# Two block sizes per step in the decay products of three recurrent heads, and reorderings in four other stages of a fused hybrid decoder layer

## The chip, the cores and the metric

The kernel runs as one program on one core of a Trainium2 chip. The metric is the device time of one execution in microseconds (us). Engines are named as the profile names them: PE is the matrix engine (TensorE), PEld its weight load, DVE the vector engine, ACT the scalar engine, POOL the GpSimd engine, SP the engine whose queue issues the DMA transfers. SBUF is the on-chip memory with 128 partitions; PSUM is the accumulator memory, eight banks of 128 x 512 f32, into which PE writes.

## The reference: what is computed

One decoder layer on x of shape 1024 x 1024 (1024 tokens, width 1024), all in f32. In the terms of the reference:

```
h = RMSNorm(x);  p = h @ W_in          # W_in: 1024 x 3584
A = dilated sliding-window attention   # 8 heads of 64, causal, table bias
R = HGRN2 recurrence                   # 4 heads of 128
x = x + RMSNorm(concat[RMSNorm(A), R] @ W_out)
x = x + RMSNorm(relu(RMSNorm(x) @ W1)^2 @ W2)    # inner width 4096
```

For each recurrent head, f_t = lb + (1 - lb) sigmoid(f_pre), k = 1 - f, and S_t = diag(f_t) S_{t-1} + k_t v_t^T, o_t = S_t^T q_t. Written without the state, token t receives from each earlier token s the product q_t . (f_{s+1} ... f_t) . k_s, channel by channel. That matrix of decayed products is what the main part of the change computes in another way. The result of the recurrence is normalised per head and multiplied by silu(gate).

## The kernel before: how it is tiled and staged

The order of all work is written out by hand. Each engine executes its own list of instructions in that order and waits at semaphores where it needs another engine. So an instruction that waits holds up everything behind it on its engine.

Products in f32 accuracy are made in three passes of a rounded format: every operand is split by `split_into` (line 81) into a high part, a copy on ACT (line 82), and a low part, a subtraction on DVE (line 83). `three_pass` (lines 86 to 88) then does high x high, low x high and high x low. Products of plain f32 operands appear in the profile as two PE records each; they are called half products here. Weights come through `w_load` and `w_split` (two raw buffers of 128 x 1024, loaded by SP).

The stages, with their time in the profiled execution:

- **Front, 0 to 56 us.** `keep_warm(n)` (line 278) issues n products of zeros, 128x256. `x_turn` (line 254) transposes a block of x on PE, ACT and DVE split it (255, 256), `x_mm` makes the first projection (value and gate of recurrent head 0) for the token groups in `groups`, into four PSUM banks `pig`. `ig_evac` (229, 230) moves a bank out: value on ACT, gate on DVE. In the trace the two take turns at a bank, each waiting for the other.
- **Recurrent heads, 56 to 325 us.** `hgrn_core(h)` computes head h. Between its parts it calls `fill(ns)`, which takes pieces of PE work from a queue of generators until their nominal cost is used up: for heads 0 to 2 the projections of the next head (`hgrn_ig`, 192 passes of 128x256, then `hgrn_qf`, 96 passes of 128x512), for head 3 an attention projection. What is left in the queue at the end of a head is issued then. The decay matrix `at` (128 x 8 x 128: eight token blocks of 128) is built by recursive halving. For each block size c in 1, 2, 4, ..., 64, `pl` is made by eight plain f32 products of 64 columns (line 392: keys x the queries in the second halves of blocks of 2c), the keys in the first halves and the queries in the second halves are multiplied by the decay over their half (396, 398), the decays are combined (402), and a predicated copy writes the 64 columns from PSUM to their places in `at` (403). Ahead of this, `pd` (377) makes the diagonal from `prod`, which the projection of f writes (367).
- **Attention, 325 to 575 us.** Steps (head, query block b): `look` makes scores and bias two steps ahead, `raise_` the exponentials one step ahead, `turn` transposes and splits, `weigh` and `finish` multiply with v. `hooks` adds work to single steps: at step 47 a transposed row block, a weight split and a bias table load. `fill` mixes in the projection of the next pair. `keys_off` (469 to 476) moves half of a pair's keys out of PSUM: one DVE multiply, two copies on ACT, two subtractions on POOL, four transfers on SP. For the second half of a pair's keys it is put off to the step with b = 7, 0 or 1 (line 875).
- **Output projection, 575 to 650 us.** A loop over eight token blocks t: `late_out`, `row_turn(t + 1)`, `residual(t - 1)`, `row_attn(t + 2)` (702, 704), `mixed_half`, `next_turn(t - 2)`, `residual_b(t - 1)`.
- **First feed-forward product, 650 to 975 us.** 1024 x 1024 x 4096 by Strassen's scheme with seven products: `mm1(q, p, ...)` (1059 to 1061) for pair q and product p, `out_p1` to `out_p7` evacuate. The operands B22, T1, T2, T4, T3 are made while pairs 0 to 4 run. `w1_sums` and `w1_split` prepare the weights of a pair, `act_plain`, `act_sums` and `act_store` form and store the activations. Buffers are handed out by small arenas (`small`, `large`), first freed, first taken.
- **Second feed-forward product, 975 to 1294 us.** 35 units of (product, pair of pairs), each of 24 passes of 128x512; `a_load(n + 3)` loads activations (1388), `prep(n + 2)` splits them. A last plain part (`fe`) adds pairs 0 and 1, and each token block is normalised, added to the residual and stored (1602 to 1622).

Of the kernel before, what the change touches and what calls it, by code (L numbers as in the profile page):

```python
# [17 lines left out]
P = 128  # L18
# [17 lines left out]
def hymba_layer(ctx, tc, x, w_in, w_out, w_ff1, w_ff2, g_pre, lb_logits, g_mix, g_post,  # L36
# [28 lines left out]
    masks = cp.tile([P, len(LEVELS), 64], U8, name="masks")  # L65
    gpre = cp.tile([P, NK], F32, name="gpre")
# [215 lines left out]
    keep_warm(3)  # L282
    for k in range(NK):
        x_turn(0, 1, k)
        keep_warm(1)
        if k == 3:
            w_split()
    w_split()
    keep_warm(2)
    for i, grp in enumerate(groups):  # L290
# [8 lines left out]
        if i == 4:  # L299
            w_split()  # L300
            ig_evac(heads[0], pms0[0], PAIRED[0])
            ig_evac(heads[0], pms0[1], PAIRED[1])
            squares(6, 2)
            rsqrt_mean(rstd0[:, 6:], ssq0[:, 6:], D, 2)
# [3 lines left out]
    V.tensor_copy(masks, mraw)  # L308
    V.tensor_tensor(out=lb, in0=lbl[:, :, 0], in1=lbl[:, :, 1], op=ALU.subtract)
# [14 lines left out]
    def hgrn_ig(h):  # L324
        hd = heads[h] = new_head(h)
        w_get(4 * h + 1)
        for t2 in range(NT // 2):
# [7 lines left out]
            ig_evac(hd, pm, (t2 * 2, t2 * 2 + 1))  # L335
# [34 lines left out]

    def hgrn_core(h, scale, after=None):
        hd = heads[h]
        inat, gate, prod, qt, kt, tot = (hd[n] for n in ("inat", "gate", "prod", "qt", "kt", "tot"))
        fill(2200 * scale)
# [8 lines left out]
        cur = tot  # L383
        fill(2300 * scale)
        for li, c in enumerate(LEVELS):
            nb = 64 // c
            qv = qt.rearrange("p (b two c) -> p b two c", two=2, c=c)
            kv = kt.rearrange("p (b two c) -> p b two c", two=2, c=c)
            av = at.rearrange("p n (b two c) -> p n b two c", two=2, c=c)
            pl = bank("s", f"pl{h}_{li}")  # L390
            for n in range(NT):
                TE.matmul(pl[:, n * 64:(n + 1) * 64], kt[:, n * P:(n + 1) * P],  # L392
                          qv[:, n * nb:(n + 1) * nb, 1, :], start=True, stop=True)
            w = T // (2 * c)
            cv = cur[:, :2 * w].rearrange("p (b two) -> p b two", two=2)
            V.tensor_tensor(out=kv[:, :, 0, :], in0=kv[:, :, 0, :],  # L396
                            in1=cv[:, :, 1:2].to_broadcast([P, w, c]), op=ALU.mult)
            V.tensor_tensor(out=qv[:, :, 1, :], in0=qv[:, :, 1, :],  # L398
                            in1=cv[:, :, 0:1].to_broadcast([P, w, c]), op=ALU.mult)
# [3 lines left out]
            V.copy_predicated(  # L403
                av[:, :, :, 1, :],
                masks[:, li].rearrange("p (b c) -> p b c", c=c).unsqueeze(1).to_broadcast([P, NT, nb, c]),
                pl.rearrange("p (n b c) -> p n b c", n=NT, c=c))
            cur = nx
            fill(2900 * scale)
# [456 lines left out]
    for s in range(n_steps):  # L865
# [9 lines left out]
        if b in (7, 0, 1):  # L875
            while put_off:
                keys_off(*put_off.pop())
# [12 lines left out]
        hooks.get(s, lambda: None)()  # L890
        fill(3400.0 - 360.0 * b if s < n_steps - 20 else 1000.0 if s < n_steps - 16 else 1300.0)
# [87 lines left out]
    def split_pair(name, src):  # L979
        hi, lo = small.get(f"{name}h", F32R), small.get(f"{name}l", F32R)  # L980
        split_into(hi, lo, src)
# [319 lines left out]
    b_split("T3", h11)  # L1301
    large.add("A")
    for q in range(2):
        out_p6(q)
# [3 lines left out]
    wide_split(2)  # L1308
    for q in range(2):
# [5 lines left out]
    w1_split(2, 2)  # L1315
    w1_load(4)
    w1_split(2, 3)
# [373 lines left out]
```

## Time and profile before

| | |
|---|---|
| median of three executions | 1299.04 us (1296.51, 1299.04, 1299.54) |
| the profiled execution | 1296.25 us, of which its span 1294.4 us |
| PE busy | 1254.5 us, 97% of the span |
| DVE busy | 857.5 us, 66% |
| ACT busy | 515.6 us, 40% |
| POOL busy | 295.5 us, 23% |
| DMA | 153.98 MB, mean 119 GB/s |

A row of the groups reads: line, engine, operation, output <- inputs, shape, number of records; then busy us and mean ns of one; then the idle time of the engine just before these instructions and who ended it. A row of the timeline reads: start in us from the beginning of the span, length in us (of the whole run of records, where it ends in x and a number), engine, line, operation, and in brackets how long the engine was idle before and who released it. In a table of windows, each engine's busy time is followed by PEclk, the share of PE's full clock that was granted.

### The profile page before, as it was taken

The numbers are of one execution on the slowest core, as the hardware profiler recorded it, in microseconds if no ns is written. First come the engines' busy times: TensorE is split into PE (matmuls) and PEld (weight loads), VectorE is DVE, ScalarE is ACT, GpSimd is POOL, SyncE is SP. The second block draws the span as 40 slices with busy tenths as digits, with TensorE's granted clock in tenths as the row PEclk, the third lists the DMA queues.
The fourth block names the chain that finished last, engine by engine and source line by source line (L and its number), as shares of the span: only waits on it lengthen the run. The fifth ranks groups of instructions, "written<-read, shape, count | busy, mean of one in ns | idle before, by whom it ended". The sixth has DMA issues, their size and how long they took to land. (4 is left out here: it accounts for less than half of the span.)

```text
span 1294.4 us, 17367 instructions
## 1 busy us (share of the span) xinstructions
PE 1254.5 (97%) x6666; PEld 1071.5 (83%) x6666; DVE 857.5 (66%) x1395; ACT 515.6 (40%) x904; POOL 295.5 (23%) x308
## 2 busy tenths in 40 slices
PE   8999999999999999899999899999999999999997
PEld 8898989988888887787877788888878888888885
DVE  5565656575665656667758566666675777688956
ACT  6612121222555555574655322222234633344412
POOL 0000000011112123134350387575541000000012
PEclk9999999999999999999999999999999999999998
DMA  5201111132223223326242345453478454434423
GB/s 204 66 17 51 33 44 38 29 86 66 82 66 82 66 82 80 127 70 221 97 148 90 138 171 179 147 179 127 142 260 333 163 195 130 156 105 131 156 75 126
DMA packets 58577, 153.98 MB, mean 119 GB/s; under 512 B 4992, under 2 KB 12928, under 8 KB 58240
## 3 DMA queue, kind: packets, MB, share of 16 engines
q1 hardware_dynamic: 58496, 152.89, 35.6%
q8 instruction: 52, 0.85, 0.3%
q14 instruction: 29, 0.24, 0.1%
HBM read 106.73 MB, written 39.85 MB: 113 GB/s over the span
## 5 line engine op out<-in xcount | busy, mean ns | idle before, releaser
L87 PE MATMUL f<-bl,ah 128*128 128x512 f32 x392 | 152.6, 389 | 0.5 <-DVE bl L83 0.5
L86 PE MATMUL f<-bh,ah 128*128 128x512 f32 x392 | 152.6, 389 | 0.0
L88 PE MATMUL f<-bh,al 128*128 128x512 f32 x392 | 152.5, 389 | 0.0
L83 DVE TENSOR_TENSOR al<-ar,ah 128x1024 fp32r<-128x1024 f32 x49 | 60.7, 1239 | 50.2 <-ACT ah L82 21.6
L87 PEld LDWEIGHTS f<-bl,ah 128*128 128x128 f32 x392 | 73.6, 188 | 16.1 <-DVE bl L83 0.8
L86 PEld LDWEIGHTS f<-bh,ah 128*128 128x128 f32 x392 | 73.6, 188 | 15.6 <-ACT acc L1471 0.4
L88 PEld LDWEIGHTS f<-bh,al 128*128 128x128 f32 x392 | 73.6, 188 | 15.1
L82 ACT ACTIVATE ah<-ar 128x1024 fp32r<-128x1024 f32 x49 | 52.3, 1067 | 53.6 <-DMA ar<-actd 28.2
L1607 POOL TENSOR_SCALAR fp<-fss 128x1 f32<-128x1 f32 x8 | 3.5, 432 | 268.3 <-ACT fd L1604 268.3
L576 DVE CUSTOM_DVE_ANT_0 p<-ps,bt 128x512 f32<-128x512 f32 (+2 forms) x84 | 44.3, 552 | 24.1 <-PE ps L574 23.9
L603 ACT ACTIVATE pth<-pt 128x512 fp32r<-128x512 f32 (+2 forms) x96 | 43.2, 486 | 41.1 <-PE pt L600 39.4
L604 DVE TENSOR_TENSOR ptl<-pt,pth 128x512 fp32r<-128x512 f32 (+2 forms) x96 | 50.2, 551 | 13.1 <-ACT pth L603 13.1
L392 PEld LDWEIGHTS pl<-qt,kt 128*128 128x128 f32 x448 | 53.7, 194 | 1.5 <-PE pm_av L88 0.9
L392 PE MATMUL pl<-qt,kt 128*128 128x64 f32 x448 | 53.8, 273 | 0.5 <-DVE qt L398 0.5
L587 ACT ACTIVATE p<-p,nm 128x128 f32<-128x128 f32 (+3 forms) x64 | 49.5, 773 | 9.2 <-DVE nm L582 6.2
L229 ACT ACTIVATE inat<-pig,rstd 128x128 f32<-128x128 f32 x32 | 11.6, 367 | 97.3 <-PE pig L88 84.2
L78 POOL TENSOR_SCALAR ms<-hss 128x8 f32<-128x8 f32 x4 | 0.8, 197 | 210.0 <-DVE hss L444 210.0
L82 ACT ACTIVATE bh<-br 128x1024 fp32r<-128x1024 f32 x28 | 29.9, 1068 | 42.6 <-PE f L88 37.3
L633 POOL TENSOR_TENSOR anat<-anat,rd 128x128 f32<-128x128 f32 x32 | 14.5, 455 | 140.4 <-DVE anat L632 136.6
L600 PE MATMUL pt<-ident,p 128*128 128x128 f32 x288 | 42.9, 276 | 3.4 <-DVE ptl L604 3.4
L1127 POOL TENSOR_TENSOR e<-x,e 128x512 f32<-128x512 f32 x14 | 20.7, 1476 | 102.0 <-DVE x L1078 102.0
L396 DVE TENSOR_TENSOR kt<-kt,tot 128x512 f32<-128x512 f32 x28 | 20.2, 722 | 35.8 <-PE pl L392 35.8
(1586 smaller groups left out, 3869.1 us busy)
## 6 DMA issues: line engine op xcount, KB each, us to landing
ar<-actd SPq DMA_DIRECT2D x49, 512.0 KB, 3.7
raw<-in_w_in_dram SPq DMA_DIRECT2D x28, 512.0 KB, 3.6
w1r<-in_w_ff_dram SPq DMA_DIRECT2D x14, 1024.0 KB, 6.5
br<-in_w_ff_dram SPq DMA_DIRECT2D x14, 1024.0 KB, 6.5
actd<-e SPq DMA_DIRECT2D x17, 768.0 KB, 4.3
actd<-e SPq DMA_DIRECT2D x11, 1024.0 KB, 4.1
xr<-in_x_dram SPq DMA_DIRECT2D x8, 512.0 KB, 8.7
raw<-in_w_out_dram SPq DMA_DIRECT2D x8, 512.0 KB, 3.7
```

The costliest lines, as they stand in the source:

```text
L82: S.activation(hi, src, AF.Copy)
L83: eng.tensor_tensor(out=lo, in0=src, in1=f32(hi), op=ALU.subtract)
L86: TE.matmul(dst, lhs[0], rhs[0], start=start, stop=False)
L87: TE.matmul(dst, lhs[0], rhs[1], start=False, stop=False)
L88: TE.matmul(dst, lhs[1], rhs[0], start=False, stop=stop)
L392: TE.matmul(pl[:, n * 64:(n + 1) * 64], kt[:, n * P:(n + 1) * P], qv[:, n * nb:(n + 1) * nb, 1, :], start=True, stop=True)
L576: V.tensor_tensor_reduce(out=pe[:, k0:k0 + n], in0=pS[:, :n], in1=bts[hd][:, o:o + n], scale=1.0, scalar=-3.0e38, op0=ALU.add, op1=ALU.max ...
L587: S.activation(pe[:, :nk], pe[:, :nk], AF.Exp, bias=nm[:, b:b + 1], accum_out=dn[:, b:b + 1])
L600: TE.transpose(pt[:, j * P:(j + 1) * P], pe[:, jj * P:(jj + 1) * P], ident)
L603: S.activation(hi, src, AF.Copy)
L604: V.tensor_tensor(out=lo, in0=src, in1=f32(hi), op=ALU.subtract)
L1127: eng[0].tensor_tensor(out=e1[:, 3], in0=a21, in1=e1[:, 2], op=ALU.add)
```

## The change

Nine edits. The parts that carry the work, first the recurrent heads 0 to 2 (head 3 keeps the old loop, with the first two `fill` calls changed as for the others):

```
+    def quarter_sets(hd, h, step, tots):
+        c = 4 ** step
+        nb = 32 // c
+        qt = hd["qt"]
+        cv = tots.rearrange("p (n b f) -> p n b f", n=NT, f=4)
+        sets = []
+        for hf in range(2):
+            q = qt[:, hf * 512:hf * 512 + 512]
+            z = slab("T", f"qs{h}_{step}{hf}", F32, (P, 4, 192))
+            n4 = slice(hf * 4, hf * 4 + 4)
+            S.activation(z[:, :, :64].rearrange("p n (g c) -> p n g c", c=c),
+                         q.rearrange("p (n g two c) -> p n g two c", n=4, two=2, c=c)[:, :, :, 1], AF.Copy)
+            z2 = z[:, :, 64:128].rearrange("p n (b two c) -> p n b two c", two=2, c=c)
+            q4 = q.rearrange("p (n b f c) -> p n b f c", n=4, f=4, c=c)
+            S.activation(z2[:, :, :, 0], q4[:, :, :, 2], AF.Copy)
+            V.tensor_tensor(out=z2[:, :, :, 1], in0=q4[:, :, :, 3],
+                            in1=cv[:, n4, :, 2:3].to_broadcast([P, 4, nb, c]), op=ALU.mult)
+            V.tensor_tensor(out=z[:, :, 128:].rearrange("p n (b w) -> p n b w", b=nb),
+                            in0=z[:, :, 64:128].rearrange("p n (b w) -> p n b w", b=nb),
+                            in1=cv[:, n4, :, 1:2].to_broadcast([P, 4, nb, 2 * c]), op=ALU.mult)
+            sets.append(z)
+        return sets, cv
     def hgrn_core(h, scale, after=None):
...
-        fill(2200 * scale)
+        ready = quarter_sets(hd, h, 0, tot) if h < HH - 1 else None
+        fill(3300 * scale)
         pd = bank("t", f"pd{h}")
...
+        if h < HH - 1:
+            fill(1200 * scale)
+            totals = slab("P", f"tot{h}")
+            for step in range(3):
+                c = 4 ** step
+                nb = 32 // c
+                sets, cv = ready
+                banks4 = []
+                for u in range(4):
+                    pl = bank("st"[u // 2], f"pl{h}_{step}{u}").rearrange("p (n q) -> p n q", n=2)
+                    for n in range(2 * u, 2 * u + 2):
+                        TE.matmul(pl[:, n % 2, :192], kt[:, n * P:(n + 1) * P], sets[u // 2][:, n % 4],
+                                  start=True, stop=True)
+                    banks4.append(pl)
+                w = T // (4 * c)
+                at_ = (0, 768, 960)[step]
+                tots = totals[:, at_:at_ + 3 * w].rearrange("p (i w) -> p i w", i=3)
+                u23, u123, nx = (tots[:, i] for i in range(3))
+                cw = cv.rearrange("p n b f -> p (n b) f")
+                q4 = qt.rearrange("p (m f c) -> p m f c", f=4, c=c)
+                k4 = kt.rearrange("p (m f c) -> p m f c", f=4, c=c)
+
+                def spread(ap, k=c):
+                    return ap.unsqueeze(2).to_broadcast([P, w, k])
+                V.tensor_tensor(out=q4[:, :, 1], in0=q4[:, :, 1], in1=spread(cw[:, :, 0]), op=ALU.mult)
+                for hf in range(2):
+                    n4 = slice(hf * 4, hf * 4 + 4)
+                    V.tensor_tensor(out=qt[:, hf * 512:hf * 512 + 512].rearrange("p (n b f c) -> p n b (f c)", n=4, f=4, c=c)
+                                    [:, :, :, 2 * c:],
+                                    in0=sets[hf][:, :, 128:].rearrange("p n (b w) -> p n b w", b=nb),
+                                    in1=cv[:, n4, :, 0:1].to_broadcast([P, 4, nb, 2 * c]), op=ALU.mult)
+                V.tensor_tensor(out=u23, in0=cw[:, :, 2], in1=cw[:, :, 3], op=ALU.mult)
+                V.tensor_tensor(out=u123, in0=cw[:, :, 1], in1=u23, op=ALU.mult)
+                V.tensor_tensor(out=nx, in0=cw[:, :, 0], in1=u123, op=ALU.mult)
+                if step < 2:
+                    ready = quarter_sets(hd, h, step + 1, nx)
+                V.tensor_tensor(out=k4[:, :, 2], in0=k4[:, :, 2], in1=spread(cw[:, :, 3]), op=ALU.mult)
+                V.tensor_tensor(out=k4[:, :, 1], in0=k4[:, :, 1], in1=spread(u23), op=ALU.mult)
+                V.tensor_tensor(out=k4[:, :, 0], in0=k4[:, :, 0], in1=spread(u123), op=ALU.mult)
+                for u, pl in enumerate(banks4):
+                    for part_, mask, c2 in ((0, masks[:, 2 * step], c), (2, masks[:, 2 * step + 1], 2 * c),
+                                            (1, near[:, step], 2 * c)):
+                        av = at[:, 2 * u:2 * u + 2].rearrange("p n (b two c) -> p n b two c", two=2, c=c2)
+                        V.copy_predicated(
+                            av[:, :, :, 1, :],
+                            mask.rearrange("p (b c) -> p b c", c=c2).unsqueeze(1).to_broadcast([P, 2, 64 // c2, c2]),
+                            pl[:, :, part_ * 64:part_ * 64 + 64].rearrange("p n (b c) -> p n b c", c=c2))
+                cur = nx
+                fill((7000, 7000, 7000)[step] * scale)
+            pl = bank("s", f"pl{h}_6")
             for n in range(NT):
-                TE.matmul(pl[:, n * 64:(n + 1) * 64], kt[:, n * P:(n + 1) * P],
-                          qv[:, n * nb:(n + 1) * nb, 1, :], start=True, stop=True)
-            w = T // (2 * c)
-            cv = cur[:, :2 * w].rearrange("p (b two) -> p b two", two=2)
-            V.tensor_tensor(out=kv[:, :, 0, :], in0=kv[:, :, 0, :],
-                            in1=cv[:, :, 1:2].to_broadcast([P, w, c]), op=ALU.mult)
-            V.tensor_tensor(out=qv[:, :, 1, :], in0=qv[:, :, 1, :],
-                            in1=cv[:, :, 0:1].to_broadcast([P, w, c]), op=ALU.mult)
-            nx = slab("P", f"tot{h}_{w}") if w > 64 else \
-                tp.tile([P, w], F32, tag=f"tot{w}", name=f"tot{h}_{w}", bufs=1)
-            V.tensor_tensor(out=nx[:, :w], in0=cv[:, :, 0], in1=cv[:, :, 1], op=ALU.mult)
-            V.copy_predicated(
-                av[:, :, :, 1, :],
-                masks[:, li].rearrange("p (b c) -> p b c", c=c).unsqueeze(1).to_broadcast([P, NT, nb, c]),
-                pl.rearrange("p (n b c) -> p n b c", n=NT, c=c))
+                TE.matmul(pl[:64, n * 64:(n + 1) * 64], kt[:, n * P:n * P + 64], qt[:, n * P + 64:(n + 1) * P],
+                          start=True, stop=True)
+            S.activation(at[:64, :, 64:], pl[:64].rearrange("p (n c) -> p n c", n=NT), AF.Copy)
+            kv, qv = (x.rearrange("p (n two c) -> p n two c", two=2, c=64) for x in (kt, qt))
+            cv = cur.rearrange("p (n two) -> p n two", two=2)
+            V.tensor_tensor(out=qv[:, :, 1], in0=qv[:, :, 1], in1=cv[:, :, 0:1].to_broadcast([P, NT, 64]), op=ALU.mult)
+            V.tensor_tensor(out=kv[:, :, 0], in0=kv[:, :, 0], in1=cv[:, :, 1:2].to_broadcast([P, NT, 64]), op=ALU.mult)
+            nx = tp.tile([P, NT], F32, tag="tot8", name=f"tot{h}_8", bufs=1)
+            V.tensor_tensor(out=nx, in0=cv[:, :, 0], in1=cv[:, :, 1], op=ALU.mult)
             cur = nx
-            fill(2900 * scale)
+            fill(3400 * scale)
```

So a step treats the block sizes c and 2c together (c = 1, 4, 16): eight products of 192 columns take the place of sixteen of 64, and twelve predicated copies of 128 columns, from four banks, the place of two of 512. Size 64 stays by itself: keys of 64 tokens, an unconditional copy on ACT. The new mask `near` is made by three small DVE operations in front. Between the steps `fill` is called with 7000 where it was called twice with 2900.

The other edits, in the order of the stages: the front; `hgrn_ig`, where the gate too is now moved out on ACT; the attention step, where put-off keys go behind `weigh`, `finish` and the hooks; the output projection; the first feed-forward product, pairs 0 to 2; the last pair's store, two units later; and the last token block, where the gain is applied to both halves after the second.

```
-    keep_warm(3)
+    keep_warm(9)
     for k in range(NK):
         x_turn(0, 1, k)
-        keep_warm(1)
-        if k == 3:
+        if k in (3, 4):
             w_split()
-    w_split()
-    keep_warm(2)
+    keep_warm(5)
...
         if i == 4:
+            ig_evac(heads[0], pms0[0], PAIRED[0])
             w_split()
-            ig_evac(heads[0], pms0[0], PAIRED[0])
...
...
-            ig_evac(hd, pm, (t2 * 2, t2 * 2 + 1))
+            for u, t in enumerate((t2 * 2, t2 * 2 + 1)):
+                S.activation(hd["inat"][:, t], pm[:, u, 0], AF.Copy, scale=rstd0[:, t:t + 1])
+                S.activation(hd["gate"][:, t], pm[:, u, 1], AF.Copy, scale=rstd0[:, t:t + 1])
...
         turn(hd, b, exped.pop(s))
-        if b in (7, 0, 1):
-            while put_off:
-                keys_off(*put_off.pop())
...
         hooks.get(s, lambda: None)()
+        if b in (7, 0, 1):
+            while put_off:
+                keys_off(*put_off.pop())
...
+        if NE <= t + 2 < NT:
+            row_attn(t + 2)
         if t > 0:
             residual(t - 1)
-        if NE <= t + 2 < NT:
-            row_attn(t + 2)
...
-    b_split("T3", h11)
+    b_open("T3")
+    for c in range(2):
+        split_into(bops["T3"][2 * c], bops["T3"][2 * c + 1], h11[:, 2 * c:2 * c + 2])
+        out_p6(c)
     large.add("A")
-    for q in range(2):
-        out_p6(q)
...
     wide_split(2)
+    wd = large.get("wd2", F32R)
+    split_into(wd[:, 0:2], wd[:, 2:4], w1raw[2][:, 2:4])
+    ops1[2]["D"] = wd
+    ops1[2][7], ops1[2][4] = halves_of((wd[:, 0:2], wd[:, 2:4]))
+    drop(w1raw.pop(2))
+    w1_load(4)
+    w1_split(2, 3)
     for q in range(2):
         out_p3(q)
     for q in range(2):
         mm1(q, 7, "b", False)
         w1_drop(q, "D")
         out_p7(q)
-    w1_split(2, 2)
-    w1_load(4)
-    w1_split(2, 3)
...
         if n == 0:
             act_sums(NPAIR - 1)
+        if n == 2:
             act_store(NPAIR - 1)
...
-            if last:
-                V.tensor_tensor(out=c, in0=c, in1=gend[:, j], op=ALU.mult)
+            if last and j:
+                for i, e in enumerate(pieces):
+                    V.tensor_tensor(out=e, in0=e, in1=gend[:, i], op=ALU.mult)
```

The zero products in front are 14 where they were 13: nine ahead of the first transposes and five behind the last, none between. The second weight split is issued after the fifth transposed block, not after the eighth.

More of the change, by code (lines that the diff above doesn't have):

```diff
@@ L65, in hymba_layer @@
     masks = cp.tile([P, len(LEVELS), 64], U8, name="masks")
+    near = cp.tile([P, 3, 64], U8, name="near")
     gpre = cp.tile([P, NK], F32, name="gpre")
@@ L308, in hymba_layer @@
     V.tensor_copy(masks, mraw)
+    first = col("lowhalf", 3)
+    V.tensor_reduce(first, mraw[:, 0:6].rearrange("p (s two) j -> p s two j", two=2)[:, :, 0], axis=AX.X, op=ALU.max)
+    V.tensor_scalar(first, first, -1.0, 1.0, op0=ALU.mult, op1=ALU.add)
+    V.tensor_tensor(out=near, in0=mraw[:, 0:6].rearrange("p (s two) j -> p s two j", two=2)[:, :, 1],
+                    in1=first.unsqueeze(2).to_broadcast([P, 3, 64]), op=ALU.mult)
     V.tensor_tensor(out=lb, in0=lbl[:, :, 0], in1=lbl[:, :, 1], op=ALU.subtract)
@@ L977, in flat, with split_pair @@
         return ap.rearrange("p a c -> p (a c)")
-    def split_pair(name, src):
+    def split_pair(name, src, eng=V):
         hi, lo = small.get(f"{name}h", F32R), small.get(f"{name}l", F32R)
-        split_into(hi, lo, src)
+        split_into(hi, lo, src, eng)
         return hi, lo
```

35 lines of the change are left out of this document (27 added, 8 removed).

## The prediction

> **What bounds the kernel now.** The busy times first: PE is busy for 97% of the span, DVE for 66%, so time goes where PE gets less to do, or where one of its few waits goes.
>
> ```profile
> PE 1254.5 (97%) x6666; PEld 1071.5 (83%) x6666; DVE 857.5 (66%) x1395; ACT 515.6 (40%) x904; POOL 295.5 (23%) x308
> ```
>
> Then the groups by form and the timeline, for what a half product costs. The step from one record to the next counts, not the length of one:
>
> ```profile
> L392 PE MATMUL pl<-qt,kt 128*128 128x64 f32 x448 | 53.8, 273 | 0.5 <-DVE qt L398 0.5
> ...
> 10.46 1.46 PE L278 MATMUL pig<-warm 128*128 128x256 f32 x6
> ...
> 72.48 1.90 PE L392 MATMUL pl<-qt,kt 128*128 128x64 f32 x16
> ```
>
> Six half products of 256 columns: (1.46 - 0.38)/5 = 0.216 us each. Sixteen of 64 columns: (1.90 - 0.27)/15 = 0.109, no cheaper than the 128-column and 1-column ones (pd x8 in 0.95). So up to 128 columns something other than the columns sets the pace.
>
> Then PE's timeline, for its waits at the places that the change touches:
>
> ```profile
> 13.29 0.38 PE L87 MATMUL pig<-wig0l,hTh 128*128 128x256 f32 x1 [0.87 <-DVE wig0l L83]
> ...
> 202.92 1.05 PE L377 MATMUL pd<-ones,prod 128*128 128x1 f32 x8 [1.02 <-DVE prod L367]
> ...
> 601.09 0.63 PE L718 MATMUL pmt<-ident,row 128*128 128x128 f32 x4 [1.49 <-DVE row L702]
> ...
> 711.52 0.47 PE L1059 MATMUL f10b<-T30h,wd0h 128*128 128x512 f32 x1 [1.37 <-DVE x L1097]
> ...
> 726.51 0.47 PE L1059 MATMUL f12d<-T40h,wd2h 128*128 128x512 f32 x1 [3.84 <-DVE x L1094]
> ```
>
> Windows, for the granted clock. Twice a wait is followed by 3.41 us at half rate, a loss of 1.7 us of PE work each:
>
> ```profile
> 137.50:140.91 3.41, 3.41 (x18) 3.41 (x18) 0.79 (x1) 0.00 (x0) 0.00 (x0) 0.50 0.54 154
> 728.01:731.42 3.41, 3.41 (x10) 2.63 (x9) 0.28 (x1) 0.00 (x0) 0.00 (x0) 0.50 0.19 68
> ```
>
> Last the timelines of DVE and ACT: the predicated copy takes 1.32 us for blocks of 1 and 2 and 0.70 to 0.74 from 4 on, one loaded operand arrives late, and at the end a multiply by the gain stands ahead of the last sum.
>
> ```profile
> 76.23 1.32 DVE L403 COPY_PREDICATED at<-masks,pl 128x512 f32<-128x512 uint8 x1
> 85.87 0.70 DVE L403 COPY_PREDICATED at<-masks,pl 128x512 f32<-128x512 uint8 x1
> ...
> 1286.05 0.68 DVE L1613 TENSOR_TENSOR acc<-acc,gend 128x512 f32<-128x512 f32 x1
> 1286.65 0.68 DVE L1602 TENSOR_TENSOR acc<-fe,acc 128x512 f32<-128x512 f32 x1
> ...
> 993.69 1.06 ACT L82 ACTIVATE ah<-ar 128x1024 fp32r<-128x1024 f32 x1 [7.63 <-DMA ar<-actd]
> ```
>
> **The change part by part.** The sum is made against the profiled execution, 1296.25 us (span 1294.4 and 1.85 around it). It is the fastest of those shown, 2.8 below the median.
>
> *Front.* x lands at once (transposes at 5.31), so nine zero products now delay it. Cold ones step 0.43 per half; before the clock opened at 7.8 some 13 of the 18 halves fit, the other 5 take 1.1: transposes from 9.1. ACT then does four copies (0.33 apart), split, copy, split: second high part ready at 12.95. DVE's low part (1.22, behind one 0.35) ends at 14.4, where PE waited until 13.29. PE works without a break from there, so +1.2. Had the clock opened 1.3 later, both versions would start about together; 2.1 earlier, the new one 1.3 later; if the pause behind the new transposes halves the clock once more, +1.7 on top. Ends: -0.3 and +2.9. [...]
>
> *Bank first, then split* (at 42 us): PE waited 0.48 for the bank; now the low weight part, behind two ACT and two DVE moves, is ready at 42.9, so -0.1. The three mask operations (about 0.7, by the 0.16 to 0.42 of rows with 8 to 256 elements) lie in 1.46 us in which DVE waits for ACT; without that cover they would cost 0.7.
>
> *Recurrent heads 0 to 2, PE.* Per head before: 7 x 16 halves x 0.111 = 12.4 us. After: 3 x 16 halves of 192 columns. Nothing shows 192; the ends are the 128- and 256-column rows, 0.112 and 0.216, and on the line between them, 0.164, gives 7.9. Size 64: 16 halves with half the weight columns, between 0.9 and 1.8, taken at 1.3. Saved: 12.4 - 9.2 = 3.2, three heads **-9.7** (ends -0.6 and -18).
>
> *Their waits.* pd waits 0.95 at 134 and 1.02 at 203 for prod, which ends about 4 us after the last f product; the fill ahead grows by 9 passes of 0.12, so both go: -2.0. With the first goes the half clock at 137.5: -1.7.
>
> *DVE in a step.* Per two sizes before: 4 multiplies of 0.69, two copies, decays: about 5.5. After, by 0.15 + 1.05 ns per element: queries 3 x 0.42, decays up to 3 x 0.42, the next sets 2 x (0.29 + 0.42), keys 3 x 0.42, and twelve copies of 128, at blocks of 1 and 2 0.44 each (a quarter of 1.17, plus 0.15), with waits among them 5.4 in all, later 4. The queries and sets lie beside the products; keys and copies come behind them, 6.5 us against 7.5 of fill. But the four banks are wanted again one by one. Counting DVE from the last f product (fr 0.2, prod 3.3, sets 6.0, w split 7.7, at 9.0, queries, decays and sets 12.7, keys 13.8) the banks are free at 15.1, 16.5, 17.9, 19.3, and PE wants them at 17.0, 17.6, 18.3, 18.9: 0.5 us of wait in head 0. In heads 1 and 2 eight gate multiplies (2.16) stand ahead of f, DVE is 1.1 late and PE waits 1.5. So **+3.5**; ends 0 and +30, by the copy's price (rival 2). The later steps have 2 us to spare. The 24 gate moves from DVE to ACT (0.37 each) lie beside 5.8 us of PE per bank. The next weights' split at the f projection, 2.4 us of DVE, now precedes the state updates (2.6); `po` comes 5.0 us after f starts, and the first state is ready at 5.2, hidden by `po`'s first half products; a further delay would be paid in full.
>
> *Keys.* One DVE multiply (0.67), two ACT copies (1.28), two POOL subtractions (2.63) and four SP transfers move behind `finish` (0.41 DVE, 0.40 POOL) for pairs 1 and 2: 0.4 later, with over 3 us until the scores read them: 0. At step 47 they also pass a transposed block (ACT 0.60, DVE 0.69), a weight split (1.06, 1.40), its SP load and the bias table's. PE's 1.03 wait at 517.8 goes, but ACT's copies now wait for DVE until 518, exponentials and pt copies come 1.4 later, and PE waits about as long for a bank at 520.5. The last transfer goes out at 522 and takes 2.5, read at 526.9. Taken 0, ends -2.5 and +1.5.
>
> *row_attn* (0.61 + 0.35) passes four residual operations (2.86): the 1.49 wait goes. Those, their POOL sums and the x2 store come 0.9 later, and with them L795 (until 604.6), which the transposes read that PE then reaches at 602.8 instead of 604.31. Taken 0, ends -1.5 and +0.5.
>
> *First feed-forward.* out_p6(0) passes T31's split (1.22 DVE): PE starts at 710.35, not 711.52; T31 is ready at 711.4, wanted 1.4 later. The wd2 split (ACT 1.05, DVE 1.22) and wf (0.6, 0.69) pass out_p3, ACT's squares and out_p7: ready at 717.5 where f12d wanted them at 722.3. What ends that wait next is out_p5, behind DVE's out_p7: 721.9, PE there at 721.1. So 726.5 becomes 722.0: **-4.5**, and the half clock at 728 goes: -1.7. Covered: w1_load(4) goes out at 717, not 711 (6.5 to land, read after 738); squares and stores of pairs 0 and 1 are 1.8 later, wanted for a buffer at 728. Ends -6.5 and -1.
>
> *Store.* Two stores (0.37 each on SP, which waited for POOL until 984.8) now follow the loads of units 4 and 5; PE's wait at 997 goes: -0.7. Buffers come free two units later, with no reader before unit 7. Ends -0.8 and +0.5.
>
> *Tail.* L1602 starts 0.60 earlier; both gain multiplies lie beside ACT and POOL (2.2 us): -0.6.
>
> Sum: 1.2 - 0.1 - 9.7 - 3.7 + 3.5 - 6.2 - 0.7 - 0.6 = -16.3, so 1296.25 - 16.3 = **1280.0 us**.
>
> **The rivals.** (1) Half products paced by columns alone: 0.216/256 is 0.84 ns per column, so 64 would step at 0.054 and two sizes at 32 x 0.054 = 1.7 against 2.6; -9.7 would become +8: 1297.7, no change. The 0.109 row speaks against it: 3 in 100. [...]
> (2) Slower: the price of a small predicated copy is per instruction. At the full 1.32 and 0.72, step 0 holds DVE 16 us, and the waits reach some 12 + 5 us per head: 1280 - 3.5 + 50 = 1326. It decides at 20 us of waits, about 1.0 us for each copy of blocks 1 and 2. Against it: multiplies of 512, 256 and 128 take 0.68, 0.42, 0.29. With smaller mishaps of the kind, 10 in 100.
> (3) 192 columns step like 256 (0.216): +9 -> 1289: 10 in 100.
> (4) The feed-forward wait moves to out_p5 and the stores and the clock still halves: 1285: 15 in 100.
> (5) Waits at the four banks vanish and size 64 is at its low end: 1275: 10 in 100. My forecast: 52.
>
> **How the numbers follow.** The forecast reaches from 1276 to 1285. With (3), (4) and (5), 1271 to 1292 holds 8 in 10 and more; rivals 1 and 2 are outside. Under 0.3% (3.9 us) cannot be told from no change. Faster 0.86, same 0.04, slower 0.10.
>
> **What would show it.** Sixteen records of 192 columns in about 2.6 us; 48 in all three steps of a head. No wait of pd; none over 1.6 at the third and fourth bank of the second step. f12d without a wait over 1. No half clock near 137 and 728. Predicated copies of 128 columns over 0.8 us would make this wrong, as would records of 192 columns over 0.2.

## The result, and the profile after

The median went from 1298.38 to 1288.72 us, a ratio of 0.9929 (95% interval 0.9917 to 0.9942): 9.7 us faster. That is inside the range of 1271 to 1292, but outside the 1276 to 1285 of the forecast itself, and little more than half of the 19 us between 1299.04 and the forecast of 1280.0. The profiled executions, 1296.25 and 1289.73 us, lie 6.5 apart: the first is faster than each of the four before, the second the slowest of the four after. The places below are taken from these two.

The first line of busy times of the kernel after:

```profile
PE 1247.8 (97%) x6524; PEld 1061.3 (82%) x6524; DVE 885.1 (69%) x1524; ACT 533.3 (41%) x967; POOL 297.8 (23%) x308
```

PE has 6.7 us less to do (1254.5 before), DVE 27.6 more. The span became 6.5 shorter, so the waits and half-rate stretches that the change was to take away were replaced by others. The timeline of PE after, first the new products, then the waits at the places of the change:

```profile
72.13 2.77 PE L425 MATMUL pl<-qs,kt 128*128 128x192 f32 x16
...
103.69 1.15 PE L465 MATMUL pl<-qt,kt 128*64 128x64 f32 x16
...
118.22 0.71 PE L533 MATMUL po<-inat,at 128*128 128x128 f32 x4 [1.13 <-DVE st L522]
...
147.38 0.92 PE L425 MATMUL pl<-qs,kt 128*128 128x192 f32 x4 [0.32 <-DVE at L457]
148.62 0.92 PE L425 MATMUL pl<-qs,kt 128*128 128x192 f32 x4 [0.31 <-DVE at L457]
149.85 0.92 PE L425 MATMUL pl<-qs,kt 128*128 128x192 f32 x4 [0.32 <-DVE at L457]
...
598.36 1.06 PE L899 MATMUL ph<-ident,esum 128*128 128x128 f32 x8 [1.92 <-DVE esum L889]
...
600.22 0.79 PE L87 MATMUL pwo<-wh,mt 128*128 128x512 f32 x1 [0.80 <-ACT mt L83]
...
715.88 0.80 PE L1155 MATMUL f12d<-T10h,ws 128*128 128x512 f32 x1 [2.55 <-DVE ws L84]
...
723.23 0.47 PE L1153 MATMUL f12d<-T40h,wd 128*128 128x512 f32 x1 [0.68 <-DVE x L1188]
```

The products of 192 columns step by (2.77 - 0.33)/15 = 0.163 us, those of 64 columns with 64 weight columns by (1.15 - 0.27)/15 = 0.059. `pd` no longer waits. But a wait of 1.13 stands ahead of `po` in heads 0 and 1, which the kernel before did not have, the 1.49 of `pmt` has become 1.92 and 0.80 at `ph` and `pwo`, and the 3.84 of `f12d` has become 2.55 and 0.68. `po` of head 0 in the kernel before:

```profile
115.76 0.60 PE L439 MATMUL po<-inat,at 128*128 128x128 f32 x4
```

Windows of the kernel after, at the place near 137 us that was at half rate before, and at the three that are at half rate now (PEclk is the number after the five engines):

```profile
137.50:140.91 3.41, 3.41 (x28) 3.41 (x27) 3.37 (x6) 1.49 (x6) 0.00 (x0) 1.00 0.57 154
517.51:524.34 6.83, 5.96 (x22) 4.87 (x21) 3.79 (x11) 2.36 (x7) 1.24 (x1) 0.50 0.82 282
599.43:606.26 6.83, 6.04 (x14) 4.73 (x15) 5.96 (x9) 2.55 (x8) 2.18 (x4) 0.50 0.08 34
715.49:718.90 3.41, 3.02 (x7) 2.44 (x8) 3.41 (x4) 0.00 (x0) 1.47 (x1) 0.50 0.00 0
```

17.1 us at half rate, where the kernel before had 10.2 and the prediction expected 3.4 to be left.

Where the 6.5 us come from, by the start of the same product in both traces (how much earlier PE gets there, place by place), and inside the heads by the steps from one PE record to the next, summed by output:

| place | predicted | traces |
|---|---|---|
| front, to the first f projection | +1.1 | -0.3 |
| heads 0 to 2: products with their bank waits (36.5 us became 30.0) | -9.7 + 3.5 = -6.2 | -6.5 |
| heads: waits of `pd`, half clock at 137 | -3.7 | -2.4 - 1.6 = -4.0 |
| heads: wait of `po` for DVE's state updates (2.3), and slower steps around it (1.5) | 0 | +3.8 |
| attention, with the keys | 0 | +0.6 |
| output projection (row_attn) | 0 | +3.2 |
| first feed-forward product | -4.5 - 1.7 = -6.2 | -1.7 |
| store | -0.7 | -1.0 |
| tail | -0.6 | -0.6 |
| sum | -16.3 | -6.5 |

### The profile page after: what moved, and what is told of

Its sections match the earlier page's. It is cut to its first block, busy times and chain, and to the rows that moved or that the text cites. A ratio compares the mean times of both kernels' runs of the same rounds, so it can differ in the third digit from the quotient of the medians.

```text
span 1287.9 us, 17288 instructions
## 1 busy us (share of the span) xinstructions
PE 1247.8 (97%) x6524; PEld 1061.3 (82%) x6524; DVE 885.1 (69%) x1524; ACT 533.3 (41%) x967; POOL 297.8 (23%) x308
## 5 line engine op out<-in xcount | busy, mean ns | idle before, releaser
L84 DVE TENSOR_TENSOR wl<-raw,wh 128x1024 fp32r<-128x1024 f32 x23 | 31.4, 1365 | 18.3 <-ACT wh L83 18.0
L694 PEld LDWEIGHTS pt<-ident,p 128*128 128x128 f32 x288 | 33.5, 141 | 9.3 <-DVE ptl L698 6.8
L711 PE MATMUL pov<-pth,v 128*128 128x256 f32 (+1 forms) x160 | 40.6, 288 | 0.0
L1574 DVE TENSOR_TENSOR acc<-f,acc 128x512 f32<-128x512 f32 x52 | 33.8, 684 | 8.3 <-PE f L89 8.3
```

The costliest lines, as they stand in the source:

```text
L84: eng.tensor_tensor(out=lo, in0=src, in1=f32(hi), op=ALU.subtract)
L694: TE.transpose(pt[:, j * P:(j + 1) * P], pe[:, jj * P:(jj + 1) * P], ident)
L711: TE.matmul(po[:, c0:256], vst, pt[j // 4][q][:, j % 4, c0:], start=j == 0 and q == 0, stop=j == nj - 1 and q == 1)
L1574: V.tensor_tensor(out=acc_at(p, i), in0=pm, in1=acc_at(p, i), op=ALU.add)
```

## The experiments

Medians of separate comparisons stand against their own runs of the kernel before, so ratios are compared: the changed kernel's is 0.9929, and 0.0010 is 1.3 us.

### The recurrent heads alone

The kernel before with this part of the change and nothing else (front, keys, output projection, feed-forward, store and tail as before).

> The kernel before with the edit of the three recurrent heads alone (the joint block sizes, the mask for them, the gate moved out on ACT, the fills); all else as before. By the places in the trace of the changed kernel, the heads became 6.6 us shorter between the first f projection (0.34 early) and the first projection of attention (6.96 early): 1298.4 - 6.6 = 1291.8. By the terms of the prediction (-9.7 - 3.7 + 3.5) it would be 1288.5. If what the heads gain were given back in the attention behind them, it would stay above 1295.

Measured: 1288.72 against 1297.49, ratio 0.9932 (0.9917 to 0.9947). In its trace the heads are 6.6 us shorter, as in the changed kernel. So by the medians the heads carry the whole gain, and the other edits together bring nothing that can be measured. By the table they sum to about zero: -0.3, -1.7, -1.0 and -0.6 against +0.6 and +3.2. The expected time was missed: the ratio is nearer to the 1288.5 by the prediction's terms than to the 1291.8 by the places. The medians lie 8.8 us apart and the heads gain 6.6 in the trace; where the other 2.2 come from stays open.

### row_attn behind the residual again

```
+        if t > 0:
+            residual(t - 1)
         if NE <= t + 2 < NT:
             row_attn(t + 2)
-        if t > 0:
-            residual(t - 1)
```

> The changed kernel with row_attn behind residual again. Theory: the edit took away a wait of 1.49 us and put two of 1.92 and 0.80 in its place, which lie together in so few us that the clock halves for 6.83 us; undone, the place 590 to 612 gets 3.1 us shorter: 1288.7 - 3.1 = 1285.6, no half clock near 600. Rival: the halving is an accident of where the window falls, and the waits alone count: 1288.3 to 1288.7.

Measured: 1286.81, ratio 0.9913 (0.9898 to 0.9928), 2.1 us below the changed kernel's ratio, where 3.1 were expected; the intervals overlap. PE's timeline there:

```profile
592.45 0.63 PE L812 MATMUL pmt<-ident,row 128*128 128x128 f32 x4 [1.51 <-DVE row L796]
595.66 1.03 PE L899 MATMUL ph<-ident,esum 128*128 128x128 f32 x8
597.11 0.50 PE L87 MATMUL pwo<-wh,mt 128*128 128x512 f32 x1 [0.42 <-ACT mt L83]
```

The wait of 1.51 is back, the one at `ph` is gone, and there is no half clock at 600. Over the stage (575 to 650 us in the kernel before) the trace gains 0.3 us where the changed kernel loses 3.2. In the seven profiles with the new order (the changed kernel and six of the runs below and above) the clock halved near 600 in five, for 3.41 or 6.83 us; in the seven with the old order in none. The edit's waits are 2.72 us where they were 1.89 (1.49 and 0.40). In the two profiles with the new order in which the clock did not halve, the place from 590 to 612 us lost 0.8 in each; in the five others, the changed kernel's among them, it lost 1.3 to 3.6. So the waits cost 0.8, and the clock makes up the rest.

### POOL's sums of pair 3 later

DVE and POOL in the changed kernel, behind `out_p6`; first DVE, then POOL:

```profile
709.38 0.69 DVE L1109 TENSOR_TENSOR ss<-ss,w1r 128x512 f32<-128x512 f32 x1
710.11 1.81 DVE L1110 TENSOR_TENSOR s<-w1r,ss 128x512 f32<-128x512 f32 x1
711.84 1.78 DVE L1111 TENSOR_TENSOR w1r<-w1r 128x512 f32<-128x512 f32 x1
713.54 2.29 DVE L84 TENSOR_TENSOR ws<-ss,ws 128x1024 fp32r<-128x1024 f32 x1
```

```profile
710.07 1.29 POOL L1108 TENSOR_TENSOR ss<-w1r 128x512 f32<-128x512 f32 x1 [33.29 <-DVE ss L1109]
711.44 1.62 POOL L1109 TENSOR_TENSOR ss<-ss,w1r 128x512 f32<-128x512 f32 x1
713.14 1.60 POOL L1110 TENSOR_TENSOR s<-w1r,ss 128x512 f32<-128x512 f32 x1
714.71 2.25 POOL L1111 TENSOR_TENSOR w1r<-w1r 128x512 f32<-128x512 f32 x1
```

In the kernel before POOL made the same sums 7 us later, when DVE worked on operands from PSUM, and DVE's four took 0.69, 0.69, 0.69 and 1.22. The last three on DVE, then POOL's first:

```profile
713.33 0.69 DVE L1016 TENSOR_TENSOR s<-w1r,ss 128x512 f32<-128x512 f32 x1
713.94 0.69 DVE L1017 TENSOR_TENSOR w1r<-w1r 128x512 f32<-128x512 f32 x1
714.54 1.22 DVE L83 TENSOR_TENSOR ws<-ss,ws 128x1024 fp32r<-128x1024 f32 x1
```

```profile
717.09 1.30 POOL L1014 TENSOR_TENSOR ss<-w1r 128x512 f32<-128x512 f32 x1 [37.11 <-PE f11b L1060]
```

Their start hangs on a buffer. The change takes `wd2` from the `large` arena, where before it took two of the `small` ones; so the next taker, the sums of pair 3, gets a small buffer that was given back earlier. The experiment hands them the third free one, which PE gives back at the same pass of f11b as before:

```
+        if q == 3:
+            small.free.insert(0, small.free.pop(2))
         ss = small.get(f"ss{q}")
```

> The changed kernel, with the sums of pair 3's weights on POOL given the third free buffer instead of the first, which PE gives back later (at the end of product 7 of pair 1). Theory: the DVE instructions with two operands in SBUF (0.69, 0.69 and 1.22 us before, 1.81, 1.78 and 2.29 after) were slow because POOL read SBUF at the same time; now they take 0.69, 0.69, 1.22 again, the wait of 2.55 us in f12d and the half clock behind it go, and the operation that sums product 5 comes 3.9 earlier: 1288.7 - 3.9 = 1284.8. Rival: they are slow for another reason (the new order): durations stay at 1.8 to 2.3 and the time at 1288.7.

Measured: 1286.47, ratio 0.9917 (0.9902 to 0.9931): 1.6 us below the changed kernel's, where 3.9 were expected; the intervals overlap. By the places the stretch from 693 to 735 us gains 4.8 us, 3.1 more than in the changed kernel. DVE in it, and POOL:

```profile
709.84 0.69 DVE L1112 TENSOR_TENSOR s<-w1r,ss 128x512 f32<-128x512 f32 x1
710.45 0.68 DVE L1113 TENSOR_TENSOR w1r<-w1r 128x512 f32<-128x512 f32 x1
711.05 1.22 DVE L84 TENSOR_TENSOR ws<-ss,ws 128x1024 fp32r<-128x1024 f32 x1
713.45 1.78 DVE L84 TENSOR_TENSOR wf<-s,wf 128x512 fp32r<-128x512 f32 x1
```

```profile
712.47 2.21 POOL L1110 TENSOR_TENSOR ss<-w1r 128x512 f32<-128x512 f32 x1 [37.20 <-PE f11b L1156]
```

The durations are back to 0.69, 0.68 and 1.22 with the order of DVE unchanged: beside POOL's sums they had been 1.07 to 1.12 us longer each, and POOL's three later sums had taken 1.60 to 2.25, where all four take 1.29 or 1.30 in the kernel before. These instructions of DVE and POOL have all their operands in SBUF. In the kernel before, the three of DVE that start beside POOL's sums (717.59, 718.20 and 718.92 us) have one operand in PSUM, and they took 0.68 and 0.69. By what means the two engines slow each other is not shown. POOL's sums now meet the split of `wf` instead, and that one takes 1.78 where it took 0.68 in the changed kernel. The wait of 2.55 is gone, and so is the half clock at 715. PE now waits 1.76 for the sum of product 5, behind `out_p7`, the place that the prediction named as the next.

### The feed-forward edit undone

> The changed kernel with the edit of the first feed-forward product undone. By the places of the trace the edit as made brought 1.7 us (3.21 early at 700, 4.91 at 730): 1288.7 + 1.7 = 1290.4, with the wait of 3.8 us and the half clock behind it as before. By the prediction's term (-6.2) it would be 1294.9.

Measured: 1292.01, ratio 0.9952 (0.9935 to 0.9968). With the wait of 3.83 and the half clock behind it back as before, the edit is worth 3.0 us in ratio, by about 2 either way: nearer to the 1.7 of the places than to the 6.2 of the prediction. The places of other profiles add a warning. Six have the edit with the wait of 2.55, and the stretch from 693 to 735 us gains 1.3 to 1.7 us in three of them and 0.0 to 0.1 in the other three, in which the clock halves for 3.41 us behind the next wait (2.08 or 2.09, for the sum of product 5).

### The weight split behind the state updates

The changed kernel, DVE ahead of `po` in head 0:

```profile
114.45 2.36 DVE L84 TENSOR_TENSOR wig2l<-raw,wig2h 128x1024 fp32r<-128x1024 f32 x2 [0.26 <-ACT wig2h L83]
116.73 0.29 DVE L520 COPY st<-pu 128x128 f32<-128x128 f32 x1
117.05 2.33 DVE L522 SCALAR_TENSOR_TENSOR st<-st,tot,pu 128x128 f32<-128x128 f32 x6
```

The experiment issues this split two passes into the f projection:

```
-        w = w_get(4 * h + 3, 2 if h + 1 < HH else 1)
+        w = w_get(4 * h + 3, 0)
...
+            for piece, cost in enumerate(proj_t(w, f"f{h}", hf, box)):
+                if hf == 0 and piece == 2:
+                    w_get(4 * h + 3, 2 if h + 1 < HH else 1)
+                yield cost
```

> The changed kernel, with the split of the next head's first two weights put behind the state updates on DVE (issued two passes into the f projection instead of ahead of it). Theory: the fills of the change add up to more than those of before, so this split (2.36 us on DVE) now comes ahead of the state updates, and the products with the state wait 1.13 us in heads 0 and 1 (1.29 with the restart) and 0.15 in head 2; behind it the waits go: 1288.7 - 2.6 = 1286.1. Rival: the wait goes but ACT and DVE are then late at the gate or at the next projection, and PE waits there as long: 1288.7.

DVE and PE in it:

```profile
114.06 0.28 DVE L523 COPY st<-pu 128x128 f32<-128x128 f32 x1
114.38 2.33 DVE L525 SCALAR_TENSOR_TENSOR st<-st,tot,pu 128x128 f32<-128x128 f32 x6
116.62 2.36 DVE L84 TENSOR_TENSOR wig2l<-raw,wig2h 128x1024 fp32r<-128x1024 f32 x2
```

```profile
116.87 0.60 PE L536 MATMUL po<-inat,at 128*128 128x128 f32 x4
```

`po` starts without a wait, and nothing takes its place in the heads: they are 9.6 us shorter than before, not 6.6. The medians show less than the 2.6 expected: 1287.27, ratio 0.9923 (0.9909 to 0.9938), 0.8 us below the changed kernel's, which its interval cannot tell from none or from 2.6. The places settle where the time was lost; the medians of this run alone do not settle how much of it reaches the end.

### More fill behind the second step

```
-                fill((7000, 7000, 7000)[step] * scale)
+                fill((8500, 7000, 5500)[step] * scale)
```

> The changed kernel with fill 8500, 7000 and 5500 behind the three steps instead of 7000 each. Theory: DVE is late by 0.4 us in head 0 and by 0.95 in heads 1 and 2 (four banks wanted one after the other) at the second step only, and has over 2 us to spare at the third; 1500 more there gives about 1.6 us of products: the waits of 0.6 + 1.4 + 1.4 us, with restarts, go: 1288.7 - 3.4 = 1285.3. Rival: the third step or size 64 then waits instead: 1287 to 1289.

Measured: 1285.55, ratio 0.9908 (0.9894 to 0.9923), 2.7 us below the changed kernel's, where 3.4 were expected; the intervals overlap. The second step of head 1 then runs through:

```profile
147.32 2.85 PE L425 MATMUL pl<-qs,kt 128*128 128x192 f32 x16
```

No other step waits. The heads are 11.1 us shorter than before, 4.4 more than in the changed kernel.

### The keys as before, the front as before

> The changed kernel with the keys moved out ahead of the products, as before. Prediction: 0. The trace has the place 500 to 530 0.6 longer in the changed kernel than in the one before, with a half clock of 6.83 us in it where there were 3.41, and the same sum of waits (5.3 and 5.4 us): 1288.7 - 0.6 = 1288.1, between 1287.5 and 1289.

Measured: 1289.56, ratio 0.9931 (0.9912 to 0.9949): no difference. The 1289.56 lies just above the expected 1287.5 to 1289. In the trace the place gains 2.2 us where the changed kernel loses 0.6, as the clock did not halve there; this execution was the slowest of four from 1285.76 to 1290.12, with half clocks at 597 and 724.

> The changed kernel with the zero products and the second weight split in front as before. Prediction's term: +1.2 for the change, so 1288.7 - 1.2 = 1287.5 with it undone. By the traces so far the first f projection starts 0.34 early to 0.56 late with the new front (nine zero products first) and 0 to 0.38 late with the old one, as the clock opens at 5.3 to 7.3 or at 7.8 to 8.4: no difference, 1288.7 within 0.5.

Measured: 1288.47, ratio 0.9924 (0.991 to 0.9938): no difference. Over eleven profiles with nine zero products first and three with the old front, the first f projection starts 0.11 late and 0.06 early on average against the kernel before, and it goes with when the clock opens, that is, when the step of a zero half product falls from 0.43 to 0.216 us: with the new front 0.43 early where it opened at 5.31, 1.07 late where it opened at 8.30. At the same opening the new front is the later one: 54.99 against 54.04 us with openings at 6.88 and 6.84, 55.66 against 54.98 with 8.30 and 8.35. It opened earlier on average, at 6.4 against 7.7 us, and that evens it out; three profiles of the old front are too few to say whether the order of the zero products is the cause.

### Four things together

row_attn as before, POOL's sums later, the split behind the state updates, and the fills.

> The changed kernel with four things together: row_attn as before, POOL's sums of pair 3 later, the weight split behind the state updates, and fills 8500, 7000, 5500. If they add: from the runs so far, in ratio to the kernel before 0.9913 and 0.9917 where the changed kernel has 0.9929, so 2.1 and 1.6 us, and 2.6 and 3.4 from the two above: 1288.7 - 9.7 = 1279.0. If the clock's gains overlap, 1281.

Measured: 1275.23, ratio 0.9832 (0.9818 to 0.9847): 12.6 us below the changed kernel's, more than the 9.7 expected. The traces show the same 12.6, by places: 7.5 in the heads, which is the 3.0 and the 4.4 of the two single traces; 3.3 in the output projection; 2.8 between 693 and 735 us; the other places lose 1.0. The 9.7 had taken 2.1 for row_attn and 1.6 for POOL's sums, from the medians.

> The kernel with the four things together (ratio 0.9832 to the kernel before), and the keys as before. With the new order a wait of 2.15 us stands close behind one of 1.34, and in 6 of 7 profiles the clock halves there for 3.4 to 6.8 us; with the old order four waits of about 1 us lie apart, and it halves for 3.4, 3.4 and 0 us in three profiles. Theory: 1.0 to 2.0 us faster, ratio 0.9817 to 0.9825. Rival: the keys' order does not matter (prediction: 0): 0.9832.

Measured: 1275.38, ratio 0.9824 (0.9811 to 0.9837), against 0.9832 with the new order: inside the theory's 0.9817 to 0.9825, but the intervals overlap, so the two are not to be told apart. In this profile the clock is full from 8.30 us to the last products.

> The kernel with the four things together, and the sum of product 5 of pair 2 on DVE ahead of the four operations of product 7 of pairs 0 and 1. In the trace of the four, PE waits 1.78 us for it at product 4 of pair 2. Theory: that wait goes, and with it the halvings that it can bring: 1.8 us faster, ratio 0.9818. Rival: the stores of pairs 0 and 1, 0.7 later, take as much back: 0.9832.

The edit issues product 5 of pair 2 and its sum between product 7 and `out_p7`:

```
     for q in range(2):
         mm1(q, 7, "b", False)
         w1_drop(q, "D")
+    mm1(2, 5, "d", True)
+    out_p5(2)
+    for q in range(2):
         out_p7(q)
```

Measured: 1274.18, ratio 0.9817 (0.9803 to 0.983): the expected 0.9818, though the interval overlaps that of the four together (0.9818 to 0.9847). In its trace the wait at product 4 of pair 2 is gone.

> Both of the last two on the four together: if they add, ratio 0.9803 to 0.9811, about 1272.5 us.

Measured: 1273.19, ratio 0.9807 (0.9794 to 0.982), as expected if the two add. This is the fastest version: about 25 us below the kernel before, 16 below the changed one by ratio. Its busy times, PE at product 4 of pair 2, and the sum on DVE that it no longer waits for:

```profile
PE 1239.1 (97%) x6524; PEld 1057.0 (83%) x6524; DVE 881.6 (69%) x1524; ACT 533.4 (42%) x967; POOL 298.0 (23%) x308
```

```profile
705.71 0.39 PE L1158 MATMUL f12d<-T40h,wd 128*128 128x512 f32 x1
```

```profile
704.20 0.68 DVE L1193 TENSOR_TENSOR x<-f12d,x 128x512 f32<-128x512 f32 x1
```

PE is busy 8.7 us less than in the changed kernel with the same 6524 records: nearly all of that is the half rate, under which a product of 512 columns lasts 0.63 us and not 0.39, in steps of 0.43 and not 0.23 (717 and 720 us of the changed kernel; 17.1 us at half rate there, none here before the last products). Its four executions lie within 0.8 us; those of the changed kernel within 2.4.

## Why the prediction was right or wrong, point by point

- **Half products.** Right, and the fear of rival 3 was not borne out: 192 columns step by 0.163, the straight line's 0.164. Size 64 was mis-sized on the safe side: 16 halves of 0.059 are 0.95 us, the low end, not 1.3. So the step in these rows is about 0.85 ns (0.92 with 64 weight columns) for each column of whichever is more, moving columns or weight columns: 128 weight columns 0.109, 64 weight columns 0.059, 192 moving 0.163, 256 moving 0.216. Rival 1 fell with the 0.109 of 64 moving columns, as argued. The records of the weight loads are longer than the steps, mostly 190 ns for 128 columns (L425) and 138 for 64 (L465).
- **The bank waits.** Right in place and size: +0.5, 1.5 and 1.5 predicted; 0.38, 0.95 and 0.95 of idle time, with restarts about 0.7, 1.4 and 1.4.
- **The predicated copies.** The timeline of DVE in the changed kernel, first step:

```profile
79.88 0.92 DVE L457 COPY_PREDICATED at<-masks,pl 128x128 f32<-128x128 uint8 x2
80.83 0.45 DVE L457 COPY_PREDICATED at<-near,pl 128x128 f32<-128x128 uint8 x1
```

  They cost 0.44 to 0.5 each, as taken (0.44). Rival 2 needed 1.0.
- **`pd` and the clock at 137.** Right: -4.0 for -3.7. The half clock of the kernel before at 137 us is that of one profile; no other run has the old heads.
- **The state behind the weight split.** Wrong. The step said that the split "now precedes the state updates (2.6)" and that "the first state is ready at 5.2, hidden by `po`'s first half products; a further delay would be paid in full". Its times were right: f starts at 111.91, the first state was ready at 117.02, 5.1 us later, and `po` was due at 117.09. But the first product of `po` has no operand among the states. It takes its bank from the pool of two in which `pu` lies, so it waits until DVE has read all of the first `pu`: the copy and three of the updates, to 118.2. Ahead of these stand the query's multiply (113.50) and the split (114.45). The step looked for the reader of the state and not for the bank. Moving the split behind the updates gives back 3.0 of the 3.8 in the heads.
- **row_attn.** Wrong, and mostly in the clock. That `ph` would be reached about 1.8 us before L795's output was ready stands in the step's own numbers, 602.8 against 604.6; the trace has 1.92, and 0.80 for `mt` behind it. The step netted the two waits to 0, where they added 0.8, and left out the clock: the stretch of 3.41 with the 1.92 in it was followed by one at half rate, and that one, with the 0.80 in it, by another. Waits and clock together are the 3.2 us.
- **The first feed-forward product.** The order did what the step said; two of its durations were wrong. It counted DVE's sums and splits at 0.69 and 1.22, from rows in which POOL stood still, and did not follow which buffer the sums of pair 3 would get. With POOL beside them they took 1.1 longer each, `ws` came 3.3 late, and the wait of 2.55 with its half clock stood where the step saw none. With POOL later the predicted next stop (the sum of product 5) shows, at 1.76. Rival 4, the wait that moves and a clock that still halves, left 1.2 of the 6.2 and was near the 1.7, with another cause.
- **Keys.** Taken 0 between -2.5 and +1.5; +0.6 in the traces, nothing in the medians. What it left out is again the clock: it halved between 505 and 530 us in eight of nine profiles with the new order and in two of five with the old one, and from 500 to 545 us the old order is 1.0 us shorter on average.
- **Front.** +1.2 was worked out for a clock that opens at 7.8. In the changed kernel's profile it opened at 5.52 and the place gained 0.3. Where it opened at 7.24 and 8.30 the loss was 0.5 and 1.1, so +1.2 was too much for 7.8 as well: between those two profiles it would be about 0.8. The step compared both fronts at one opening of the clock and left out that the opening itself differs, so the term should not have entered a forecast of medians with its full weight.
- **Store and tail.** Right: -1.0 and -0.6 for -0.7 and -0.6.
- **The sum.** The terms that failed, +3.8, +3.2 and 4.5 of the feed-forward's 6.2, are 11.5 us; the front (1.4 better) and small ones give back 1.7. Three of these places are the same mistake: a wait that goes was priced, the next instruction's wait was seen or looked for, but not the clock, the bank or the engine beside it. That the total still lies inside the range is partly luck: the traces show 6.5 of the 16.3 us, two fifths. The median stays within the range because its upper part had been given to rivals (3) and (4), 1289 and 1285, and neither of these came as described.
- **The rivals' sums.** The +9 of rival 3 is not the step of 192 columns alone: 144 halves at 0.052 more are 7.5, and the rest needs size 64 at its high end. The +30 at the end of the bank waits falls short of the 50 that rival 2 works out for the same cause. Neither bears on the result.

## What the runs showed of the hardware that was not expected

**The clock halved behind stretches with 1.92 us of idle time or more.** Its steps lie on one grid: in the changed kernel it opens at 5.52 us, and half rate begins at 517.51, 599.43 and 715.49, which is 150, 24 and 34 times 3.413 us further on each time. Windows on this grid, first of the changed kernel, then of the one with row_attn as before; idle time of PE is the length less the first busy time:

```profile
712.07:715.49 3.42, 1.26 (x6) 0.72 (x4) 3.42 (x2) 1.58 (x2) 3.34 (x3) 1.00 0.00 0
715.49:718.90 3.41, 3.02 (x7) 2.44 (x8) 3.41 (x4) 0.00 (x0) 1.47 (x1) 0.50 0.00 0
```

```profile
705.89:709.30 3.41, 2.06 (x10) 1.37 (x8) 3.41 (x3) 0.98 (x2) 3.25 (x3) 1.00 0.00 0
709.30:712.71 3.41, 2.22 (x10) 1.84 (x11) 3.41 (x3) 0.59 (x2) 2.29 (x2) 1.00 0.00 0
```

Both are the same wait of 2.55 us. In one, 2.16 of it lie in a single stretch and the next is at half rate; in the other a border of the grid cuts it into 1.35 and 1.19, and the clock stays. Over the fourteen profiles, all 18 stretches at full rate with 1.92 us of idle time or more were followed by half rate (2.18 at 523.21 us of the kernel before, and 2.14, 1.93 and 2.16 at 514.10, 596.02 and 712.07 of the changed one, are among them). Of the two next in order, just under 1.92 (at 721.18 and 724.59 us of the kernel before), the second was, and of those with less only four: with 0.95 (among the one-column products of `pd`), 1.50, 1.77 and 1.82 us. So idle time is not all that counts, and what else does is not shown. From half rate it came back after a stretch with at most 0.45 idle and stayed after 0.73 and more (0.39 at 715.49, and 0.87 and 0.79 at 517.51 and 599.43, in the changed kernel). 1.92 us are 56% of a stretch of 3.41.

**So the price of this wait depended on where the grid fell:** 3.41 us at half rate followed it in the one profile and none in the other. Four executions of one kernel spread by up to 4.4 us (1285.76 to 1290.12), while those of the version with no wait over 1.6 spread by 0.8. That fits; that the clock makes the spread is not shown, as only one execution of each kernel has a trace.

**The predicated copies cost mostly by the element, with a surcharge for blocks of 1 and 2:** 128 elements took 0.44 to 0.5 there and about 0.30 from blocks of 4 on, where 512 took 1.32 and 0.70 to 0.74.

## What to carry to other kernels

Where PE waits, ask for the sum of idle time within 3.4 us and not for the single wait: in the changed kernel the waits of 1.92 and 0.80 us close together had 6.83 us at half rate behind them, by an estimate up to 3.4 us of PE's work (half of 6.83), and the 1.13 us ahead of `po` in heads 0 and 1, alone in their stretches, had none. When a reordering lets another engine start earlier, follow the buffer that releases it, and look whether it and DVE then work on SBUF at the same time: here DVE's 0.69 and 1.22 us became 1.81 and 2.29 beside POOL, and the durations of the profile before did not hold. And when more background work is drained ahead, what it brings along for the other engines (here a split of 2.4 us on DVE) moves ahead too, past something that PE is about to wait for.
